# A short first transfer ahead of the first tile's load in a 1-D average pool

## The chip, the cores and the metric

The kernel runs on one core of a Trainium2 chip. The metric is device time in microseconds (us), the median over a few runs. Before the change the three runs took 333.34, 333.50 and 333.92 us, so the median is 333.5 us.

The core has several engines with their own instruction streams. Here VectorE (DVE in the profile), GpSimd (POOL) and ScalarE (ACT) compute, SyncE (SP) issues all transfers, and the transfers themselves are carried out by the core's 16 DMA engines.

## The reference

The input `x` has shape 32 x 256 x 4096 in float32, which is 134.2 MB. The output has 256 columns for each of the 32 x 256 = 8192 rows, which is 8.4 MB. Each output is the mean of 16 neighbouring inputs of its row:

```python
for i in range(output_size):
    start = int(i * length / output_size)
    end = int((i + 1) * length / output_size)
    result[:, :, i] = np.mean(x[:, :, start:end], axis=-1)
```

## The kernel before

**Tiling.** The 8192 rows are dealt out over 128 partitions, four rows to a partition and tile, so there are 16 tiles (`ntiles`) of 128 x 16384 float32, 8.39 MB each. Within the first 15 tiles a partition owns 60 consecutive rows of the input (`x_many`), and tile t is their t-th group of four: for each partition one contiguous stretch of 64 KB. The last tile has a view of its own (`x_last`). One transfer loads one tile, with one stretch of 64 KB per partition.

**Buffers.** `inpool` has two buffers, so the load of tile t+2 can only be issued when the work on tile t has ended. The results stay on the chip in `res_many` (15 tiles) and `res_last` (1 tile) until the end.

**Work on a tile.** Each tile is split in two halves of 512 windows. GpSimd adds, in the second half, the upper eight inputs of each window to the lower eight (L78). VectorE meanwhile sums the 16 inputs of each window of the first half (L83), and then, after GpSimd, the eight sums that are left of each window of the second half (L86). ScalarE scales the 1024 results by 1/16 (L89).

**Order of the transfers.** All of them are issued by SP on one queue, in the order of the program: 16 loads (L75), then `res_many` to the output in one transfer of 7.86 MB, then `res_last` in two (120 partitions, then 8), all from the helper `store` (L58). The framework puts the waits: a load waits until VectorE and GpSimd are through with its buffer. The second load also waits for a VectorE memset (L74) of the first 1536 elements of its buffer, which the load then overwrites. Transfers on the queue are carried out while SP goes on, so up to two loads are under way or queued at a time.

**What the change touches.** It touches only L75 for t = 0, the very first transfer of the program. The consumers of that tile are L78 (second half of the tile), L83 (first half) and L86.

Of the kernel before, what the change touches and what calls it, by code (L numbers as in the profile page):

```python
# [1 line left out]

# [4 lines left out]


@with_exitstack
def kernel(  # L10
    ctx: ExitStack,
    tc: tile.TileContext,
    x: bass.AP,
    output_size: int,
    out: bass.AP,
):

    nc = tc.nc
    F32 = mybir.dt.float32
    X = mybir.AxisListType.X

    batch, channels, length = x.shape
    ob, oc, olen = out.shape
    assert ob == batch and oc == channels and olen == output_size
    assert length % output_size == 0
    window = length // output_size  # L30
    hw = window // 2
    inv_w = 1.0 / float(window)

    P = nc.NUM_PARTITIONS
    R = 4
    rows = batch * channels
    assert rows % (P * R) == 0
    ntiles = rows // (P * R)
    many = (ntiles - 1) * R
    cells = R * output_size  # L40
    m = cells // 2
    cols = R * length

    xr = x.rearrange("b c l -> (b c) l")
    orow = out.rearrange("b c o -> (b c) o")
    x_many = xr[0 : P * many, :].rearrange("(p r) l -> p (r l)", p=P, r=many)
    o_many = orow[0 : P * many, :].rearrange("(p r) o -> p (r o)", p=P, r=many)
    x_last = xr[P * many :, :].rearrange("(p r) l -> p (r l)", p=P, r=R)
    o_last = orow[P * many :, :].rearrange("(p r) o -> p (r o)", p=P, r=R)

    res_many = nc.alloc_sbuf_tensor("res_many", [P, (ntiles - 1) * cells], F32, align_bytes=256)
    res_last = nc.alloc_sbuf_tensor("res_last", [P, cells], F32, align_bytes=256)
    inpool = ctx.enter_context(tc.tile_pool(name="inpool", bufs=2))

    stored = nc.alloc_semaphore("stored")

    def store(out, in_):
        ins = nc.sync.dma_start(out=out, in_=in_)  # L58
        tc.no_tile_sem_insts.add(ins.ins.name)
        ins.then_inc(stored, 16)  # L60

    for t in range(ntiles):
        last = t == ntiles - 1
        xbuf = inpool.tile([P, cols + 64], F32, name="xin")
        off = 32 if last else 0
        flat = xbuf[:, off : off + cols]
        xin = flat.rearrange("p (o w) -> p o w", w=window)
        if last:
            res, base, src = res_last, 0, x_last
        else:  # L70
            res, base = res_many, t * cells
            src = x_many[:, t * cols : (t + 1) * cols]
        if t == 1:
            nc.vector.memset(flat[:, 0:1536], 0.0)  # L74
        nc.sync.dma_start(out=flat, in_=src)  # L75
        if last:
            store(o_many, res_many[:, :])
        nc.gpsimd.tensor_add(  # L78
            out=xin[:, m:cells, 0:hw],
            in0=xin[:, m:cells, 0:hw],  # L80
            in1=xin[:, m:cells, hw:window],
        )
        nc.vector.reduce_sum(  # L83
            out=res[:, base : base + m], in_=xin[:, 0:m, :], axis=X
        )
        nc.vector.reduce_sum(  # L86
            out=res[:, base + m : base + cells], in_=xin[:, m:cells, 0:hw], axis=X
        )
        nc.scalar.mul(  # L89
            out=res[:, base : base + cells],  # L90
            in_=res[:, base : base + cells],
            mul=inv_w,
        )
    for lo, hi in ((0, 120), (120, P)):
        store(o_last[lo:hi, :], res_last[lo:hi, :])

    ctx.pop_all().close()
    tc.close()
    tc.compile()  # L99
    nc.sync.wait_ge(stored, 48)  # L100
    nc.sync.sem_clear(stored)


# [1 line left out]
_INS = ['x', 'output_size']  # L105
_OUTS = [((32, 256, 256), 'float32')]

_NUMBERS = {'output_size': 256}


# [26 lines left out]
```

## Time and profile before

| What | Value |
|---|---|
| time, median of 3 runs | 333.5 us (333.34 to 333.92) |
| span of the profiled execution, first to last instruction | 332.3 us |
| time of the profiled execution itself | not recorded apart from the three runs; the median lies 1.2 us above the span |
| VectorE busy | 211.0 us (64%) |
| GpSimd busy | 139.7 us (42%) |
| ScalarE busy | 18.2 us (5%) |
| DMA queue q1 | 142.61 MB, 99.4% of 16 engines' span |
| first load: issued by SP, first consumer starts | 0.74 us, 22.69 us |
| second load: issued by SP, first consumer starts | 2.49 us, 42.03 us |
| last tile's first consumer starts | 313.02 us |

The span counts from the program's first instruction to its last. Engine times are sums over instructions and overlap each other. The DMA share is the time that the transfers' packets took, over 16 engines. A packet here is a contiguous piece that one DMA engine moves: for the loads one partition's 64 KB, eight of them per engine and tile. In tables by windows a packet counts whole in the window in which it starts, so shares over 1 appear in short windows; the rate in GB/s divided by the packet's size gives the number of packets that started there.

### The profile page before, as it was taken

Reading aid. Unit: us, or ns where it says so; the run is one execution under the profiler, and the core shown is the slowest. Engines: PE = TensorE matmul, PEld = TensorE weight load, DVE = VectorE, ACT = ScalarE, POOL = GpSimd, SP = SyncE. Lnnn points to the kernel's source line nnn. Section 1 sums busy time; section 2 is a strip of 40 time slices with the busy share of each in tenths; the row PEclk is TensorE's granted clock in tenths of the full one; section 3 lists DMA queues with packets and bytes.
Section 4 is the critical chain, followed back from the end, with each engine's and each line's share of the span. In section 5 each row is a group of like instructions: output and inputs, shape, how many; then the busy total and the mean of one; then the engine's idle time right before and its main releaser. Section 6 shows DMA issues by size and latency. Waiting matters only on the chain.

```text
span 332.3 us, 162 instructions
## 1 busy us (share of the span) xinstructions
DVE 211.0 (64%) x33; ACT 18.2 (5%) x17; POOL 139.7 (42%) x20
## 2 busy tenths in 40 slices
DVE  1029396692939669392956939295683929578392
ACT  1000101001010100001010000101000010101001
POOL 0027091642709164370906437090633709063370
DMA  9898999989898999989898998989899898989897
GB/s 379 379 505 379 489 394 442 442 379 505 379 505 379 489 394 394 489 379 505 379 497 387 426 458 379 505 379 505 379 481 402 387 497 379 505 379 505 363 473 300
DMA packets 2599, 142.61 MB, mean 429 GB/s; under 512 B 295, under 2 KB 295, under 8 KB 423
## 3 DMA queue, kind: packets, MB, share of 16 engines
q1 hardware_dynamic: 2599, 142.61, 99.4%
HBM read 134.22 MB, written 8.39 MB: 429 GB/s over the span
## 4 chain that ended last, share of the span: by engine, by line
DMA 65%; POOL 18%; DVE 11%; POOLq 3%; issue 0%; ACT 0%
DMA xin<-in_x_dram 65%; POOL xin L78 18%; DVE res_many L86 9%; POOLq L99 3%; DVE res_last L86 1%; DVE xin L74 0%; ACT res_last L89 0%; POOLq L78 0%
## 5 line engine op out<-in xcount | busy, mean ns | idle before, releaser
L78 POOL TENSOR_TENSOR xin<-xin 128x4096 f32<-128x4096 f32 x16 | 139.5, 8717 | 181.9 <-DMA xin<-in_x_dram 181.9
L83 DVE TENSOR_REDUCE res_many<-xin 128x512 f32<-128x8192 f32 x15 | 130.3, 8686 | 105.0 <-DMA xin<-in_x_dram 105.0
L86 DVE TENSOR_REDUCE res_many<-xin 128x512 f32<-128x4096 f32 x15 | 66.3, 4420 | 2.4 <-POOL xin L78 2.3
L89 ACT ACTIVATE res_many<-res_many 128x1024 f32<-128x1024 f32 x15 | 15.8, 1056 | 289.7 <-DVE res_many L86 289.7
L83 DVE TENSOR_REDUCE res_last<-xin 128x512 f32<-128x8192 f32 x1 | 8.7, 8686 | 6.6 <-DMA xin<-in_x_dram 6.6
L86 DVE TENSOR_REDUCE res_last<-xin 128x512 f32<-128x4096 f32 x1 | 4.4, 4422 | 0.2 <-POOL xin L78 0.2
L89 ACT ACTIVATE res_last<-res_last 128x1024 f32<-128x1024 f32 x1 | 1.1, 1056 | 18.8 <-DVE res_last L86 18.8
L74 DVE MEMSET xin<- 128x1536 f32 x1 | 1.3, 1338 | 1.1 <-PEq L118 1.1
L89 ACT ACT_TABLE_LOAD x1 | 1.3, 1283 | 0.7 <-PEq L118 0.7
L118 POOL MEMSET const-float32-0.0<- 128x1 f32 x1 | 0.1, 98 | 0.2 <-issue 0.2
L118 POOL MEMSET const-bfloat16-1.0<- 128x1 bf16 x1 | 0.1, 101 | 0.0
L118 POOL MEMSET const-uint8-127<- 128x1 uint8 x1 | 0.1, 101 | 0.0
L118 POOL MEMSET const-float32-1.0<- 128x1 f32 x1 | 0.1, 98 | 0.0
## 6 DMA issues: line engine op xcount, KB each, us to landing
out_dram<-res_many SPq DMA_DIRECT2D x1, 7680.0 KB
out_dram<-res_last SPq DMA_DIRECT2D x1, 480.0 KB
xin<-in_x_dram SPq DMA_DIRECT2D x16, 25.3
out_dram<-res_last SPq DMA_DIRECT2D x1, 32.0 KB
```

Source lines behind the costliest of these rows:

```text
L74: nc.vector.memset(flat[:, 0:1536], 0.0)
L78: nc.gpsimd.tensor_add(out=xin[:, m:cells, 0:hw], in0=xin[:, m:cells, 0:hw], in1=xin[:, m:cells, hw:window],)
L83: nc.vector.reduce_sum(out=res[:, base : base + m], in_=xin[:, 0:m, :], axis=X)
L86: nc.vector.reduce_sum(out=res[:, base + m : base + cells], in_=xin[:, m:cells, 0:hw], axis=X)
L89: nc.scalar.mul(out=res[:, base : base + cells], in_=res[:, base : base + cells], mul=inv_w,)
L99: tc.compile()
L118: nc = _bacc.Bacc("TRN2", target_bir_lowering=False, num_devices=1)
```

## The change

The load of the first tile becomes two transfers on the same queue. The first brings columns 0 to 127 (512 bytes) of each partition, 64 KB in all; the second, issued directly behind it, brings columns 128 to 16383 (65,024 bytes) of each partition. The other 15 loads are as before.

```diff
-        nc.sync.dma_start(out=flat, in_=src)
+        if t == 0:
+
+            nc.sync.dma_start(out=flat[:, 0:128], in_=src[:, 0:128])
+            nc.sync.dma_start(out=flat[:, 128:cols], in_=src[:, 128:cols])
+        else:
+            nc.sync.dma_start(out=flat, in_=src)
```

In the instruction streams SP has 23 rows in place of 22. The first reduce of tile 0 waits for both transfers, GpSimd's add on tile 0 for the second one alone (its half begins at column 8192), and the third load, which reuses the buffer, waits for both as well. The completion semaphores are dealt out in turn, so all later transfers move on by one semaphore. Nothing else changes place.

## The prediction

> **What bounds the kernel now.** I read the page's DMA rows first, because the busiest engine is only at 64%.
>
> ```profile
> DVE 211.0 (64%) x33; ACT 18.2 (5%) x17; POOL 139.7 (42%) x20
> ...
> DMA  9898999989898999989898998989899898989897
> ...
> q1 hardware_dynamic: 2599, 142.61, 99.4%
> ```
>
> The 16 DMA engines are busy for 99.4% of the span, in every slice. The question is then whether any engine's work ever holds a transfer up. The chain of work that ended last seems to say so, since it passes through GpSimd and VectorE. The timeline around the third load and the chain's end tell otherwise.
>
> ```profile
> 35.94 0.33 SPq L75 DMA_DIRECT2D xin<-in_x_dram  x1
> ...
> 42.03 8.72 POOL L78 TENSOR_TENSOR xin<-xin 128x4096 f32<-128x4096 f32 x1 [10.57 <-DMA xin<-in_x_dram]
> ...
> 327.42 0.75 SPq L58 DMA_DIRECT2D out_dram<-res_last  x2
> ```
>
> The third load is issued at 35.94, when tile 0's work ends, but the second load occupies the DMA engines until just before 42.03. So 6.1 us of queued work lie between the release of a buffer and the moment the queue would run dry. At the end the last results are issued at 327.42, while the store of `res_many` still runs. The chain names who releases whom. It does not say that the transfers ever stop.
>
> The third view is the table by windows, which shows the stream of transfers at its beginning, in the middle and at its end. The columns are the window, its length, busy time of DVE, ACT and POOL, a clock, the DMA share, and GB/s.
>
> ```profile
> 1.70:2.70 1.00, 0.76 (x1) 0.32 (x1) 0.00 (x0) 1.00 3.06 1049
> 2.70:4.70 2.00, 0.00 (x0) 0.00 (x0) 0.00 (x0) 1.00 0.00 0
> 4.70:4.90 0.20, 0.00 (x0) 0.00 (x0) 0.00 (x0) 1.00 4.54 1966
> 4.90:5.10 0.20, 0.00 (x0) 0.00 (x0) 0.00 (x0) 1.00 4.54 1966
> 5.10:5.30 0.20, 0.00 (x0) 0.00 (x0) 0.00 (x0) 1.00 1.51 655
> 5.30:5.50 0.20, 0.00 (x0) 0.00 (x0) 0.00 (x0) 1.00 1.51 655
> ...
> 42.00:311.00 269.00, 183.48 (x28) 14.78 (x14) 122.04 (x14) 1.00 1.00 433
> 330.10:332.20 2.10, 0.00 (x0) 0.00 (x0) 0.00 (x0) 1.00 0.62 250
> ```
>
> A packet counts in the window where it starts. Between 1.70 and 2.70, 1049 KB start, which is 16 packets of 64 KB, one per engine. Their share 3.06 over 16 engines is 49.0 us, or 3.06 us each. The second packets start between 4.70 and 5.50, in groups of 6, 6, 2 and 2 (1966 GB/s times 0.2 us over 64 KB is 6), and share times 16 engines times 0.2 us over 6 gives 2.42 us each. From 42 to 311 the rate is flat at 433 GB/s. So each engine runs without a break from its first packet on. Its first packet costs 3.06 - 2.42 = 0.64 us more than every other: call that the start's excess. The last window holds the 128 rows of 4096 bytes of `res_last`: 0.62 x 16 x 2.10 / 128 = 0.163 us each.
>
> So the end is the beginning of the stream plus a fixed amount of work, and a change at the beginning shows in full at the end.
>
> **The change part by part.** The sum is made against the profiled span of 332.3 us. The median of the runs is 333.5, so 1.2 us lie around the span. I take them as unchanged and add each result to 333.5.
>
> *Compute and waits, cost nothing.* Tile 0's first reduce (L83) now waits for two transfers and L78 for the second one. Both wait for about the same moment as before, 22.7 us. Even a microsecond later is covered by the 6.1 us above, because only the third load's issue depends on it. That load waits for both transfers, which have landed long before. If the cover were gone, the delay would pass one to one. Nothing is moved past another queue. ACT and POOL issue no transfers, and all instructions behind are the same. The second load waits for the memset until 2.49. SP's added issue ends at about 1.5 (below), so the second load and all later issues keep their times.
>
> *The added issue.* The first issue takes 403 ns, the typical one 328 (the rows of L75: 327/328/403 min, median, max). The bulk of tile 0 is issued 0.40 us later than now. Now the first packets start at 1.94 in the mean (groups of 4, 4, 5, 2 and 1 in finer windows from 1.70 to 2.70), and 1.94 + 0.64 = 2.58 is where their steady rate begins in effect. The mean start of the second packets, 5.0, less 2.42, says the same. The bulk's descriptors would be there at 1.94 + 0.40 = 2.34.
>
> *What moves out of the bulk.* Each engine has 8 rows of 512 bytes fewer, 4096 of 524,288 bytes per tile: 2.42 x 4096 / 65,536 = 0.15 us less.
>
> *The short rows.* No row of 512 bytes stands in this trace. The lower bound is by bytes, 0.019 us each, 0.15 us for eight. The upper bound is the nearest row however long, the 4096-byte one, 0.163 us each, 1.30 us for eight. A 4096-byte row takes 0.163 where its bytes at the bulk's rate take 0.151, so a row has 0.012 us of its own. I take 0.019 + 0.012 = 0.031 us, near the lower end, because the small fixed part is what the two measured sizes agree on: 0.25 us for eight.
>
> *The start's excess.* Either the short transfer pays it while the bulk is still being issued, or the bulk pays it, or both do. The bounds are a saving of 0.64 less what is uncovered, and 0.64 paid twice. I take the middle: it is a delay counted from an engine's first packet, paid once. The short rows then start at 1.94, are through at 1.94 + 0.64 + 0.25 = 2.83, and the bulk, there since 2.34, runs from 2.83 in place of 2.58. That is +0.25, less 0.15 for the bytes: **+0.10 us, 333.6 us**. If instead the bulk alone pays the excess from its own arrival, it is 0.40 - 0.15 = +0.25 us, 333.75. Both are inside what can be told from no change here, 0.2% or 0.67 us.
>
> *Where a rule speaks against the change.* In the row above, tiles follow each other at an unbroken 433 GB/s, although each is a transfer of its own. That shows a transfer's fixed cost hidden when the next is already queued, as it would be 0.4 us behind the first. The Trainium skill, "DMA: Bandwidth & Descriptors", section Rules for kernel authors, advises joining small transfers and says that under 64 KB one pays mostly overhead, and its section Measured gives 0.95 us of moving time for 64 KB. An estimate by that page would put the short rows' end at 1.94 + 0.95 = 2.89, the sum at +0.16 us. Its fixed cost of about 2 us for a transfer (section Anatomy of one DMA) would, if it were not hidden, make it about 335.5. The trace's unbroken rate speaks for hidden.
>
> **The rivals.**
>
> *Slower: short rows are dear.* If a short row costs what a 4096-byte row costs, the sum is 1.30 - 0.15 = +1.15 us, 334.65. It decides from 0.10 us a row (8 x 0.10 - 0.15 = 0.67). The far end is that each of the eight rows, being the first touch of its stretch of memory, pays the excess that only the first pays now: 8 x 0.64 - 0.15 = +5.0 us, 338.5. For it: a stretch's first touch has never stood on the path except at the start, since later ones lie behind a packet of 2.42 us. Against it: 4096-byte rows ran at the bulk's rate at the end, though those are stores. Chance 0.16, and 0.02 of it for the far end.
>
> *Slower: the excess is paid twice.* The bulk starts behind 2.83 and pays 0.64 again: 3.47 against 2.58, less 0.15, +0.74, 334.25. For it: nothing shows what the excess is. If it comes from sixteen engines starting large pieces at once, a small piece does not use it up. Chance 0.12.
>
> *Slower: the bulk waits for the short transfer to land.* Issue to first packet takes 1.0 us (0.74 to 1.74). Counted from 2.83, with the excess again, that is 4.47 against 2.58, less 0.15: +1.7, 335.2. Against it speaks the unbroken rate across transfers. Chance 0.05.
>
> *Faster: the short transfer takes the excess.* Then the bulk runs at its full rate from its arrival, 2.34 against 2.58, less 0.15: -0.39 us, 333.1, still within 0.2%. It passes 0.67 only if the engines also come even. The last two engines start their second packet at about 5.4, 0.4 us behind the mean, and if the slowest engine sets the end, its steady rate begins in effect at 2.98. If all begin at 2.34, that is -0.64 - 0.15 = -0.79, 332.7. For it: the first packets that start last (one in 2.30:2.70) bear little excess, so part of it is over by then and a later bulk may not meet it. Against it: the 0.40 us of issue is lost first. Chance 0.25 for passing 0.67.
>
> *Hidden anyway.* That the change has no effect because tile 0's consumers still wait for both parts holds for the consumers, and is part of the forecast. The first piece feeds nobody earlier.
>
> **How the numbers follow.** The likeliest single case, no difference over 0.67 us, holds 0.42 and contains -0.39, +0.10 and +0.25; it gives 333.6, with its own range 333.0 to 334.1. Faster has 0.25 (332.7), slower 0.16 + 0.12 + 0.05 = 0.33 (334.25, 334.65, 335.2). The range of 332.7 to 334.8 takes in both bounds of the short rows' price short of the far end, the excess paid twice, and the even start. What is left out is the wait for the landing, the far end, and a part of the faster case. The runs themselves scatter by 0.58 us, so the ends cannot be drawn closer.
>
> **What the changed profile would show.** The step of the issue: a second SP issue at about 1.15 and the third, behind the memset, still at 2.49. The short rows: 64 KB more in small packets, 128 of them, starting between 1.7 and 2.7; their mean is 0.03 us beyond the excess if I am right, 0.16 if the first rival is. The excess: the mean of the sixteen first long packets is about 2.4 to 2.5 us if the short ones took it, 3.0 if not. The end: the second tile's first consumer, now at 42.03, moves by what the start has won or lost, and so does the last tile's, now at 313.02. I am wrong if those two move by more than 0.7 us either way. If they stay and the time moves, the cause lies outside all of these steps: in the rate between (433 GB/s now) or behind the last load.

## The result, and the profile after

The changed kernel takes 333.98 us (median of 21 runs, 333.65 to 334.23), the kernel before 333.50 us (median of 21 runs, 333.34 to 333.92). The ratio is 1.0014, with a 95% interval of 1.0008 to 1.0020: slower by about 0.48 us, clear of the measurement's noise in this comparison, and inside the 0.2% that the prediction took as no change. The profiled execution has a span of 332.8 us, 0.5 us more than before, and its own time was 334.13 us.

The page's engine and DMA rows of the changed kernel:

```profile
DVE 211.0 (63%) x33; ACT 18.2 (5%) x17; POOL 139.7 (42%) x20
...
q1 hardware_dynamic: 2743, 142.61, 99.2%
...
xin<-in_x_dram SPq DMA_DIRECT2D x1, 64.0 KB, 2.0
```

The engines' work is the same to 0.1 us. The queue moves the same 142.61 MB in 144 more packets: 128 short rows and 16 of under 512 bytes, one more for each engine. Its share falls by 0.2 of a point: 99.4% of 332.3 us before and 99.2% of 332.8 now are 330.3 and 330.1 us, so the 0.5 us lie where the DMA engines move nothing. The last row says that the short transfer landed 2.0 us after its issue.

The timeline of the changed kernel shows the start and how far the consumers of the second and of the last tile moved:

```profile
0.74 0.41 SPq L77 DMA_DIRECT2D xin<-in_x_dram  x1
...
1.20 0.42 SPq L78 DMA_DIRECT2D xin<-in_x_dram  x1
2.49 34.36 SPq L80 DMA_DIRECT2D xin<-in_x_dram  x2
...
42.67 8.72 POOL L83 TENSOR_TENSOR xin<-xin 128x4096 f32<-128x4096 f32 x1 [10.62 <-DMA xin<-in_x_dram]
...
313.56 8.72 POOL L83 TENSOR_TENSOR xin<-xin 128x4096 f32<-128x4096 f32 x1 [10.86 <-DMA xin<-in_x_dram]
```

The long transfer (L78) is issued at 1.20, 0.46 us after the short one. The second tile's first consumer starts at 42.67 in place of 42.03, 0.64 us later, and the last tile's GpSimd add at 313.56, 0.43 us later than this line of the kernel before:

```profile
313.13 8.72 POOL L78 TENSOR_TENSOR xin<-xin 128x4096 f32<-128x4096 f32 x1 [11.15 <-DMA xin<-in_x_dram]
```

So a loss of the size that the time shows is still there when the last tile arrives.

The table by windows of the changed kernel, with the same columns as before:

```profile
1.80:1.90 0.10, 0.10 (x1) 0.10 (x1) 0.00 (x0) 1.00 0.37 108
1.70:2.70 1.00, 0.76 (x1) 0.32 (x1) 0.00 (x0) 1.00 2.57 846
2.70:3.50 0.80, 0.00 (x0) 0.00 (x0) 0.00 (x0) 1.00 0.89 325
3.50:5.30 1.80, 0.00 (x0) 0.00 (x0) 0.00 (x0) 1.00 0.00 0
5.30:5.50 0.20, 0.00 (x0) 0.00 (x0) 0.00 (x0) 1.00 6.07 2601
5.50:5.70 0.20, 0.00 (x0) 0.00 (x0) 0.00 (x0) 1.00 3.00 1300
5.70:6.00 0.30, 0.00 (x0) 0.00 (x0) 0.00 (x0) 1.00 1.50 650
6.00:6.20 0.20, 0.00 (x0) 0.00 (x0) 0.00 (x0) 1.00 0.75 325
42.00:311.00 269.00, 183.48 (x28) 14.78 (x14) 122.05 (x14) 1.00 1.00 433
```

- *A short row.* From 1.80 to 1.90, 108 GB/s x 0.1 us is 21 rows of 512 bytes, and 0.37 x 16 x 0.1 = 0.59 us of engine time: 0.028 us each. Eight take 0.22 us.
- *The first long packets.* From 1.70 to 3.50 the share is 2.57 x 16 x 1.0 + 0.89 x 16 x 0.8 = 52.5 us. Less 128 x 0.028 for the short rows, 48.9 us are left for 16 long packets, 3.06 us each. A 65,024-byte packet takes 2.40 us later (5.50:5.70: 3.00 x 16 x 0.2 / 4). The excess is 0.66 us, as large as before, and the long packets pay it although short ones ran ahead of them.
- *The shift.* The second long packets start in groups of 8, 4, 3 and 1, at a mean of 5.58, taking the middle of each window. Before they started at 5.00. That is 0.58 us late. The seven packets of each engine that are then still to come are 512 bytes shorter, which gives back 0.13 us: +0.45 us at the end of tile 0. The second tile's consumer moved further because it waits for the slowest engine, whose second packet starts between 6.00 and 6.20, before between 5.30 and 5.50.
- *Behind it.* The rate from 42 to 311 us is 433 GB/s, as before. One GB/s of it would be 0.6 us, so the finer sign is the last tile's consumer, 0.43 us late: what the start lost in the mean is not made up.

So the changed kernel has its bulk running 0.58 us late and gets 0.13 back. Two things remained to be tested: whether the late issue, and not the short transfer as such, is the cause, and when a leading piece covers it.

### The profile page after: what moved, and what is told of

Read it like the earlier page. It is cut to its first block, busy times and chain, and to the rows that moved or that the text cites. A ratio compares the mean times of both kernels' runs of the same rounds, so it can differ in the third digit from the quotient of the medians.

```text
span 332.8 us, 164 instructions
## 1 busy us (share of the span) xinstructions
DVE 211.0 (63%) x33; ACT 18.2 (5%) x17; POOL 139.7 (42%) x20
## 2 busy tenths in 40 slices
DMA packets 2743, 142.61 MB, mean 428 GB/s; under 512 B 311, under 2 KB 439, under 8 KB 567
## 3 DMA queue, kind: packets, MB, share of 16 engines
q1 hardware_dynamic: 2743, 142.61, 99.2%
## 4 chain that ended last, share of the span: by engine, by line
DMA 65%; POOL 18%; DVE 11%; POOLq 3%; issue 0%; ACT 0%
DMA xin<-in_x_dram 65%; POOL xin L83 18%; DVE res_many L91 9%; POOLq L104 3%; DVE res_last L91 1%; DVE xin L74 0%; ACT res_last L94 0%; POOLq L83 0%
```

## The experiments

Every comparison below is with the kernel before, run beside it on the same chip: 333.46 us for the long transfer first, ScalarE's queue, two short transfers and 8192 bytes; 333.52 for 2048 bytes, the delay by 64 elements and the two kernels without the memset; 333.50 for 1024 bytes, the two longer delays and the changed kernel once more. Theory A says that the loss is the stretch in which the engines have nothing to move, because the bulk's issue stands behind another one. Its rivals are named with each run.

### The long transfer first

```diff
-            nc.sync.dma_start(out=flat[:, 0:128], in_=src[:, 0:128])
             nc.sync.dma_start(out=flat[:, 128:cols], in_=src[:, 128:cols])
+            nc.sync.dma_start(out=flat[:, 0:128], in_=src[:, 0:128])
```

> The two transfers of tile 0 change places: the long one is issued first, the 512-byte rows behind it. Theory A (the time went into issuing the long transfer 0.46 us later on SP): the long one is issued at 0.74 again, the short rows cost 8 x 0.027 = 0.22 us against 0.15 us of bytes taken out, so +0.07 us, ratio about 1.0002, and the second tile's first consumer starts near 42.1. Theory B (the short rows or a second transfer as such cost it, wherever they stand): as the changed kernel, about +0.5 us, ratio 1.0014.

Measured: 333.49 us, ratio 1.0001 (0.9993 to 1.0010). Same transfers, same short rows, only the order is changed, and the loss is gone. Timeline:

```profile
0.73 0.40 SPq L77 DMA_DIRECT2D xin<-in_x_dram  x1
1.19 0.42 SPq L78 DMA_DIRECT2D xin<-in_x_dram  x1
...
42.14 8.72 POOL L83 TENSOR_TENSOR xin<-xin 128x4096 f32<-128x4096 f32 x1 [10.74 <-DMA xin<-in_x_dram]
```

Here L77 is the long transfer. The second tile's consumer is at 42.14, near the 42.1 that theory A gave, and not at 42.67. Theory B falls: a second transfer, or the short rows, cost nothing that can be told here as long as they stand behind.

### The short transfer on ScalarE's queue

```diff
-            nc.sync.dma_start(out=flat[:, 0:128], in_=src[:, 0:128])
+            nc.scalar.dma_start(out=flat[:, 0:128], in_=src[:, 0:128])
             nc.sync.dma_start(out=flat[:, 128:cols], in_=src[:, 128:cols])
```

> The short transfer is issued by ScalarE's queue, the long one by SP, both at about 0.74 us. Theory A: SP's issue of the long one is no longer late, so the sum is +0.07 to +0.1 us, ratio about 1.0003, first long packets start at a mean of about 1.95 and the 0.64 us excess stays. Theory B (the short piece in front disturbs the start): +0.4 to +0.5 us, ratio about 1.0013. If the short rows running ahead took the excess, the time would fall below the kernel before by up to 0.6 us.

Measured: 333.54 us, ratio 1.0001 (0.9992 to 1.0010). That fits theory A on the time. The start was not the one expected, though: read in windows of 0.2 us, the second long packets start at a mean of 5.23, 0.23 us later than before, so a part of the delay may be left that the time does not show. The page shows why the short rows did not simply run ahead:

```profile
q1 hardware_dynamic: 2599, 142.54, 99.2%
q10 hardware_dynamic: 144, 0.07, 0.1%
...
xin<-in_x_dram ACTq DMA_DIRECT2D x1, 64.0 KB, 15.0
```

The short transfer now has a queue of its own (q10) and lands 15.0 us after its issue, in place of 2.0. By the Trainium skill, "DMA: Bandwidth & Descriptors", section Queues, rings and completion order, an engine takes turns between queues packet by packet. The trace agrees, with one row to a turn, where that section of the Trainium skill gives 9 to 17 descriptors, each the order for one move, as typical for a packet:

```profile
1.70:2.75 1.05, 0.76 (x1) 0.73 (x1) 0.00 (x0) 1.00 2.43 833
2.75:4.70 1.95, 0.00 (x0) 0.00 (x0) 0.00 (x0) 1.00 0.25 102
4.80:5.80 1.00, 0.00 (x0) 0.00 (x0) 0.00 (x0) 1.00 2.43 1049
```

The first two rows add up to 1074 KB, which is the 16 first long packets and about 65 short rows: half of the 128 ran ahead of the first long packets or just behind them. In the last row, 1049 KB is one long packet and one short row for each of the 16 engines. So the other four rows of an engine take a turn of about 2.42 us each, and so does the small packet that ends the transfer on each engine (q10 has 16 packets besides the 128 rows): five turns are 12.1 of the 15.0 us.

### Two short transfers ahead

```diff
             nc.sync.dma_start(out=flat[:, 0:128], in_=src[:, 0:128])
-            nc.sync.dma_start(out=flat[:, 128:cols], in_=src[:, 128:cols])
+            nc.sync.dma_start(out=flat[:, 128:256], in_=src[:, 128:256])
+            nc.sync.dma_start(out=flat[:, 256:cols], in_=src[:, 256:cols])
```

> Two short transfers of 512-byte rows ahead of the long one. Theory A: the long one is issued at 0.74 + 2 x 0.46 = 1.66, so twice the loss, +0.9 to +1.0 us, ratio about 1.0028, first long packets start at a mean of about 3.1. Rival: the loss is paid once for having a short piece in front at all (another shape of the start), +0.5 us, ratio 1.0014.

Measured: 334.19 us, ratio 1.0020 (1.0012 to 1.0029), +0.73 us. The value lies between the two expectations and the interval holds both, so the time alone does not decide. The profile does: the long transfer (L79 here) is issued at 1.66, and its packets can be read in the windows below it.

```profile
1.66 0.42 SPq L79 DMA_DIRECT2D xin<-in_x_dram  x1
...
2.60:3.70 1.10, 0.00 (x0) 0.00 (x0) 0.00 (x0) 1.00 2.89 953
3.70:5.90 2.20, 0.00 (x0) 0.00 (x0) 0.00 (x0) 1.00 0.00 0
5.90:6.50 0.60, 0.00 (x0) 0.00 (x0) 0.00 (x0) 1.00 4.02 1720
```

The sixteen first long packets start from 2.60 on, the sixteen second ones between 5.90 and 6.50, where the changed kernel had them between 5.30 and 6.20. The long transfer has been put back a second time, as theory A has it. By the middle of that window it is 1.2 us behind the kernel before, which less 0.26 us of bytes (seven packets of each engine, 1024 bytes shorter) would be about +0.9. The interval of the time reaches to +0.97, so the +0.73 measured does not speak against it.

### Larger first pieces: 8192, 2048 and 1024 bytes

```diff
-            nc.sync.dma_start(out=flat[:, 0:128], in_=src[:, 0:128])
-            nc.sync.dma_start(out=flat[:, 128:cols], in_=src[:, 128:cols])
+            nc.sync.dma_start(out=flat[:, 0:2048], in_=src[:, 0:2048])
+            nc.sync.dma_start(out=flat[:, 2048:cols], in_=src[:, 2048:cols])
```

The other two have 512 and 256 in place of 2048.

> The first piece has 8192 bytes per partition. Its eight rows take about 8 x 0.31 = 2.5 us, longer than the second issue. Theory A: the later issue is hidden behind them and only eight more rows are paid (8 x 0.012 = 0.1 us): +0.1 us, ratio 1.0003; the first 16 packets of 8192 bytes carry the start's excess, and those of 57344 bytes none. Rival A2 (the first long packets of the second transfer pay the 0.64 us excess whatever runs before them): +0.1 to +0.7 us with the excess seen on the 57344-byte packets, ratio up to 1.002.

> The first piece has 2048 bytes per partition. Its eight rows take 8 x (0.076 + 0.012) = 0.70 us, a little more than the 0.57 us by which the long packets start later in the changed kernel. Theory A (the loss is the stretch in which the engines have nothing to move): the stretch is covered, +0.1 to +0.2 us, ratio 1.0003 to 1.0006. Rival (a short piece in front costs 0.5 us whatever its size, up to some large size): ratio 1.0014.

> The first piece has 1024 bytes per partition, between the changed kernel's 512 and the 2048 that lost nothing measurable. Theory A: the long packets start 0.57 us later, 8 x 1024 bytes per engine (0.30 us at the bulk's rate) are out of the way: +0.27 us, ratio 1.0008. Rival (any short piece costs the same until it is long): 1.0014 as the changed kernel beside it.

Measured: 333.56 us, ratio 1.0002 (0.9993 to 1.0010), with 8192 bytes; 333.58 us, 1.0003 (0.9994 to 1.0011), with 2048; 333.79 us, 1.0009 (1.0001 to 1.0018), with 1024. The last is what theory A gave (+0.27, measured +0.29), but the changed kernel run beside it came out at 333.80 (below), so 512 and 1024 bytes are not told apart. With 8192 and 2048 bytes no loss can be told, though the intervals reach to 1.0010 and 1.0011; where between 512 and 2048 the loss fades is not shown.

With 8192 bytes the windows show who pays the excess:

```profile
1.70:2.45 0.75, 0.75 (x1) 0.32 (x1) 0.00 (x0) 1.00 1.15 175
...
2.52:2.60 0.08, 0.00 (x0) 0.00 (x0) 0.00 (x0) 1.00 0.25 102
4.80:5.30 0.50, 0.00 (x0) 0.00 (x0) 0.00 (x0) 1.00 4.41 1901
```

In the first window 16 rows start (175 x 0.75 / 8.192), 1.15 x 16 x 0.75 / 16 = 0.86 us each. A later one (second row) takes 0.32. So the first rows of 8192 bytes carry 0.54 us of excess. In the last window start the 16 long packets and four short rows: (4.41 x 16 x 0.5 - 4 x 0.32) / 16 = 2.13 us for 57,344 bytes, which at the steady rate take 2.12. The long packets carry none. Rival A2 falls.

With 2048 bytes the excess is shared:

```profile
1.70:2.65 0.95, 0.76 (x1) 0.31 (x1) 0.00 (x0) 1.00 0.75 213
2.65:3.30 0.65, 0.00 (x0) 0.00 (x0) 0.00 (x0) 1.00 4.35 1654
```

In the second row start the 16 long packets and 29 short rows (1654 x 0.65 = 1075 KB). Less 0.09 us for each of these rows (the estimate of the expectation, 0.076 + 0.012), the long packets took (4.35 x 16 x 0.65 - 29 x 0.09) / 16 = 2.66 us, where 63,488 bytes at the steady rate take 2.34. That is about 0.32 us of excess, half of what they carry behind 512-byte rows. So the excess is paid once, by whatever first fills the stream, and a longer leading piece takes more of it.

### The late issue alone, without a second transfer

```diff
+        if t == 0:
+            nc.vector.memset(flat[:, 0:64], 0.0)
         if t == 1:
             nc.vector.memset(flat[:, 0:1536], 0.0)
```

The other two clear 384 and 1536 elements. Each lets the first load wait for VectorE, as the second one does anyway.

> One transfer per tile, as in the kernel before; the first load alone is issued later, because it waits for a VectorE memset of 64 elements of its buffer, which ends at about 1.2 us. Theory A: the loss is the late issue and nothing else, so a load issued 0.46 to 0.5 us later costs 0.46 to 0.5 us, ratio about 1.0015, with no short transfer at all. Rival (the short transfer's descriptors or its completion are part of the loss): less than the delay, ratio 1.0005 or below.

> One transfer per tile; the first load waits for a memset of 384 elements of its buffer and is issued at about 1.20, the time of the second issue in the changed kernel (with 64 elements it was 0.96, 0.22 us late, and the time rose by 0.19). Theory A (a late start of the stream is paid one to one, whatever the cause): +0.46 us, ratio 1.0014. Rival (the short transfer carries part of the loss itself): clearly less than the changed kernel beside it.

> The same with 1536 elements: the first load is issued at about 2.18, 1.44 us late. Theory A: +1.44 us, ratio 1.0043. If part of a late start were made up later in the stream, less, and the three delays (0.22, 0.46, 1.44) would not lie on one line.

The issues did not fall where the expectations had set them (0.96 in place of about 1.2, 1.28 of 1.20, 2.49 of 2.18), since VectorE began at 0.82, 0.88 and 1.13. Read from the timelines:

| Clears | First load issued | Later by | Time | More than before | Ratio |
|---|---|---|---|---|---|
| nothing (before) | 0.74 us | - | 333.5 us | - | - |
| 64 elements | 0.96 us | 0.22 us | 333.71 us | 0.19 us | 1.0005 (0.9996 to 1.0014) |
| 384 elements | 1.28 us | 0.54 us | 334.07 us | 0.57 us | 1.0017 (1.0008 to 1.0025) |
| 1536 elements | 2.49 us | 1.75 us | 335.29 us | 1.79 us | 1.0055 (1.0041 to 1.0068) |

```profile
0.96 1.96 SPq L77 DMA_DIRECT2D xin<-in_x_dram  x2
...
1.28 1.96 SPq L77 DMA_DIRECT2D xin<-in_x_dram  x2
...
2.49 0.40 SPq L77 DMA_DIRECT2D xin<-in_x_dram  x1
...
43.76 8.72 POOL L80 TENSOR_TENSOR xin<-xin 128x4096 f32<-128x4096 f32 x1 [10.58 <-DMA xin<-in_x_dram]
```

The first line is from the timeline with 64 elements, the second from that with 384 (both take in the second load), the last two from that with 1536 elements: there the second tile's consumer is at 43.76, 1.73 us after the 42.03 of before. The interval with 64 elements takes in no change at all; the other two show that a late start of the stream is paid one to one, and there is no short transfer in these kernels at all. The changed kernel issues its bulk 0.46 us late. On this line that costs as much, and up to 0.15 us of bytes that have gone ahead come back.

### Without the memset ahead of the second load

```diff
-        if t == 1:
-            nc.vector.memset(flat[:, 0:1536], 0.0)
```

> The kernel before without the memset that holds the second load until 2.49; it is then issued at about 1.2, right behind the first load. Theory A: the second load's packets queue behind eight packets per engine and change nothing, ratio 1.000. Rival C (a transfer issued close behind another disturbs the first one's start, which would be part of the changed kernel's loss): slower by 0.2 us or more, ratio 1.0006 or above.

> The changed kernel without the memset; the second tile's load is issued at about 1.66, while the long transfer of tile 0 has not started. Theory A: as the changed kernel, ratio about 1.0014. Rival C: slower than the changed kernel by 0.2 us or more, ratio 1.002 or above.

Measured: from the kernel before 333.49 us, ratio 1.0000 (0.9991 to 1.0009); from the changed kernel 333.87 us, ratio 1.0010 (1.0001 to 1.0019). Where the second load is issued makes no difference that can be told. Rival C finds no support: neither median shows its price of 0.2 us, though the intervals do not exclude one of that size.

### The changed kernel once more

> The changed kernel itself, as the measure for the other three on the same chip: +0.48 us, ratio 1.0014, by theory A 0.57 - 0.15 = +0.42 us.

Measured: 333.80 us, ratio 1.0011 (1.0002 to 1.0020), +0.30 us. With the first comparison (+0.48) and the changed kernel without its memset (+0.35), the three medians put the loss between 0.3 and 0.5 us. The +0.45 worked out from the trace is inside.

None of these kernels beats the kernel before by anything that can be told.

## Why the prediction was right, and which term was off

The forecast was 333.6 us, no difference over 0.2%, in a range of 332.7 to 334.8. The time is 333.98, inside the range, and the difference is 0.14%. That no difference over 0.2% came is due to the width of that limit more than to the sum: the sum gave +0.10 us and +0.48 was measured, and 0.67 us takes in both readings of the excess. The consumers of the second and the last tile moved by 0.64 and 0.43 us, the first of them just short of the 0.7 that the prediction had set as the sign of being wrong.

- *What bounds the kernel* holds. Delays of 0.22, 0.54 and 1.75 us at the first load came out as 0.19, 0.57 and 1.79 us, so the beginning of the stream shows in full at the end.
- *Compute and waits* cost nothing, as forecast: the engines' busy times are unchanged, and the third load still has its 6 us of queue ahead of it (issued at 36.52, while the second tile arrives until about 42.6).
- *The added issue* was taken as 0.40 us, from the length of one issue. From start to start two issues stand 0.46 us apart, since 0.05 us pass between them. The second packets came 0.58 us later in all. The remaining 0.1 us need not be the short transfer's own: read in windows of 0.2 us in the same way, the single late loads, issued 0.54 and 1.75 us later, have their second packets 0.64 and 1.79 us later. It is no larger than what profiled executions differ by (5.08 in place of 5.00 without the memset, where the first load is the same), so its cause stays open.
- *What moves out of the bulk*, 0.15 us, holds by bytes. *The short rows* were taken as 0.031 us and took 0.028.
- *The start's excess* is the step that failed. The prediction let it run from an engine's first packet, short or long, so that the short rows would use it up while the bulk was being issued; that made +0.10 us of the sum. The trace has 0.66 us on the first long packets (3.06 us each, where the prediction had set 3.0 as the sign that the short rows did not take it) and 0.028 us on the short rows. The other reading, written beside it as +0.25 us, "the bulk alone pays the excess from its own arrival", is the one that happened. With the measured shift in place of 0.40, and the bytes that are still to come behind it, it gives 0.58 - 0.13 = +0.45.
- *The rivals.* Dear short rows fall (0.028 us, where it decided from 0.10), and with them the dear first touch: 128 stretches were touched for the first time at that price. The excess is not paid twice (0.66 once). The bulk did not wait for the short transfer to land, which took 2.0 us from 0.74, until about 2.74: the long packets' mean start is 5.58 - 3.06 = 2.52. The faster case fell with the excess. The Trainium skill, "DMA: Bandwidth & Descriptors", section Anatomy of one DMA, gives a fixed cost of about 2.0 us for a transfer that GpSimd issues. This one was issued by SP, and its 2.0 us from issue to landing are near that; the time shows that they are hidden when the next transfer is already queued. The prediction's estimate that put the short rows' end at 2.89 takes a figure of the same page of the Trainium skill (section Measured) that is also for transfers issued by GpSimd; in the trace the last row ends at 2.41.
- *Two slips in the sums* change nothing: 8 x 0.10 - 0.15 is 0.65 and not 0.67, so that rival decides from just above 0.10 us a row, and the middles of the windows give 1.96 and not 1.94 for the mean start of the first packets.

## What to carry to other kernels

In a kernel like this one, whose transfers never pause, what delays the first large transfer is paid one to one, so issue it first and put small ones behind it: the same short piece cost 0.3 to 0.5 us ahead and nothing that could be told behind. A small piece can go ahead without a visible loss when it keeps the engines busy until the next transfer arrives, here 0.6 us: 2 KB per partition was enough, 512 bytes (0.22 us) were not. To see it, compare when the second packet of each engine starts: by then the start-up cost that the first one can hold is paid.

## What the runs showed of the hardware that I had not expected

- The start's excess does not go with an engine's first packet, nor with the first touch of a stretch of memory. Eight rows of 512 bytes ran at 0.028 us each with none of it, and the long packets behind them paid 0.66 us. Behind rows of 2048 bytes the long packets paid about 0.32 us. With rows of 8192 bytes the first ones paid 0.54 us (0.86 against 0.32), and the long packets paid nothing. What it consists of stays open.
- A short transfer on a queue of its own does not overtake. Issued by ScalarE at the same moment as the long one by SP, its 64 KB landed after 15.0 us, against 2.0 us ahead of it on one queue: half of its rows went one to a turn between packets of 64 KB.
